# The y products of two scan chunks issued together, and one PSUM bank moved from the projections to y while the scan runs

## The chip, the cores and the metric

The kernel runs on one core of one Trainium2 chip. The metric is the device time of one execution in microseconds; where several runs are given, it is their median. The core has a matrix engine (TensorE, PE in the profile; its weight loads are listed apart as PEld), VectorE (DVE), ScalarE (ACT), GpSimd (POOL) and SyncE (SP), which here issues nearly all DMA transfers. Each engine takes its instructions in a fixed order and waits on semaphores. PSUM, into which TensorE writes, has eight banks of 512 fp32 columns by 128 partitions.

## The reference, cut to what matters

One inference step of a layer: 1024 prompt tokens and 8 decode tokens (1032 columns in all), D_MODEL 1024. One input projection gives z, the x/B/C channels of a Mamba-2 mixer, dt, a pooling input and two gates. The mixer's chunked scan is the part that the change touches (8 groups of 4 heads, head size 64, state size 128, 8 chunks of 128 tokens):

```python
def step(h, inp):
    xc, dtc, bc, cc = inp
    acum = jnp.cumsum(dtc * a_gr, axis=1)
    seg = acum[:, :, None] - acum[:, None, :]
    decay = jnp.exp(jnp.where(causal, seg, -jnp.inf))
    cb = jnp.einsum('bign,bjgn->bijg', cc, bc)
    m = cb[..., None] * decay * dtc[:, None]
    y = jnp.einsum('bijgr,bjgrp->bigrp', m, xc)
    y = y + jnp.einsum('bign,bgrpn->bigrp', cc, h) * jnp.exp(acum)[..., None]
    w_end = jnp.exp(acum[:, -1:] - acum) * dtc
    h_new = h * jnp.exp(acum[:, -1])[..., None, None] + jnp.einsum('bjgr,bjgn,bjgrp->bgrpn', w_end, bc, xc)
    return h_new, y
```

After the scan: a gated norm, a pooling branch, two branch projections merged by the gates, an output projection, and a SwiGLU FFN, with norms around both.

## The kernel before, in words

Activations lie transposed, channels on the partitions and tokens along the free axis. Every large product is done as three products of two-part operands (`mm3`, lines 229 to 232: wh by xh, wh by xl, wl by xh). A *unit* (`in_unit`) is one output block of 128 channels for one third of the tokens (344 columns): eight contraction tiles by three products, 24 matmuls into one PSUM bank with the tag "pj". Its bank is read out by ScalarE (and, for z, by VectorE as well).

The order of the work: the input norm and the pooling branch (four groups of two blocks, `pool_proj` and `pool_mix`, the latter with short units of six matmuls); then eight groups of projections (`group_proj`: B, C, x0, x1 with a causal convolution on VectorE, z0 and z1; 18 units per group); then the gates (48 units); then branches, output projection and FFN. `interleave` puts one step of the scan of group g-1 behind each unit of group g; the scan of the last group runs behind units of the gates.

The scan of a group (`ssd`) has 18 steps u. Step u=2c runs `stage1(c)`: three transposes and the product of B and C into a bank with the tag "T"; from it ScalarE copies BT, and VectorE makes xdt, wx and CB. The tile E of the chunk (128 by 4 by 128) is loaded by a DMA that SP issues (line 681), goes through ScalarE (lines 683 and 685) and is multiplied by CB on VectorE (line 686). Step u=2c+3 runs `stage2(c)`: the state product (line 703) and two products with the state of the chunk before (line 705) into the one bank "S", and the four y products (xdt of a head as weights, 64 columns; E of that head as moving operand; line 709) into the one bank "y". One y bank holds two chunks, an even one and the odd one behind it: it is taken at the even chunk, and VectorE reads it at the odd one (line 724, once for each of two blocks of 128 channels; GpSimd then adds the tile eA at line 728). In the trace each fp32 product is two instructions, so a chunk has 2 of line 703, 4 of line 705 and 8 of line 709.

The PSUM banks are fixed for the whole kernel: pj 4, T 2, S 1, y 1. The scan's SBUF tiles rotate over fixed numbers of buffers: E 3, all others 2, except a few small ones with 1. A new tile in a buffer waits for the last reader of the old one. The order of instructions on an engine is made by the framework's scheduler at build time, mostly that of the program, with later instructions moved up where its own timing model has a gap.

Of the kernel before, what the change touches and what calls it, by code (L numbers as in the profile page):

```python
# [8 lines left out]
F32 = mybir.dt.float32  # L9
# [4 lines left out]
PSUM = bass.MemoryType.PSUM  # L14
DRAM = bass.MemoryType.DRAM

P = 128
SEQ = 1024
NS = 8
T = SEQ + NS  # L20
# [4 lines left out]
R = 4  # L25
# [59 lines left out]
def layer_kernel(ctx: ExitStack, tc: tile.TileContext, xT, wi, wdt, wpool, wba, wbb, wo, wfi,  # L85
# [3 lines left out]
    sync, act, dve, pool, pe = nc.sync, nc.scalar, nc.vector, nc.gpsimd, nc.tensor  # L89
# [2 lines left out]
    rp = ctx.enter_context(tc.tile_pool(name="rp", bufs=NR))  # L92
    wp = ctx.enter_context(tc.tile_pool(name="wp", bufs=2))
    dram = ctx.enter_context(tc.tile_pool(name="scr", bufs=1, space=DRAM))
    ps = ctx.enter_context(tc.tile_pool(name="ps", bufs=2, space=PSUM))

    def row(n=T, dt=F32, name="row"):
        return rp.tile([P, n], dt, name=name, tag="R")

    def bank(tag):  # L100
        return ps.tile([P, 512], F32, name=tag, tag=tag, bufs={"pj": 4, "T": 2, "S": 1, "y": 1}[tag])

# [1 line left out]
    plan = []  # L104

    def want(key, src, n=1024, eng=dve, rows_=False, raw=None):
# [80 lines left out]
        w_dma()  # L187
        return raw

# [1 line left out]
    x_rows = [row(name="xrow") for _ in range(KT)]  # L191

    def load_x(th):
# [32 lines left out]
    def pcol(base, i):  # L226
        return ppt[:, base + i:base + i + 1]
# [3 lines left out]
        pe.matmul(out, wh, xl, start=False, stop=False)  # L231
        return pe.matmul(out, wl, xh, start=False, stop=stop)  # L232

# [1 line left out]
    def sum_cols(bk, src, toks=TOK, c0=0):  # L235
        for i, off in enumerate(toks):
            pe.matmul(bk[:, c0 + i:c0 + i + 1], src[:, off:off + P], ones[:, 0:1], start=True, stop=True)
# [28 lines left out]
    def rstd_bank(bk, scale, eps):  # L266
        return rstd_spread(rstd_diag(bk, scale, eps))

# [1 line left out]
    xh = [None] * KT  # L270
    xl = [None] * KT

# [11 lines left out]
    def in_rstd(sacc):  # L284
        bk = bank("T")
        sum_cols(bk, sacc)
        return rstd_diag(bk, 1.0 / 1024, eps1)
# [32 lines left out]
    def load_in(blk):  # L320
        return load_w("in", blk)

# [1 line left out]
    s_yb = dram.tile([KT, P, T], F32, name="s_yb")  # L324
    icnt = const.tile([P, 16], F32, name="icnt")
    for t in range(15):
# [94 lines left out]
                act.activation(out=yb[:, TH[th]], in_=pt[:, :W], func=AF.Copy, scale=pcol(PP_PSC, blk))  # L421
            sync.dma_start(out=s_yb[blk], in_=yb)

# [1 line left out]
    dtT = const.tile([P, 9, 32], F32, name="dtT")  # L425
    wend = const.tile([P, 8, 32], F32, name="wend")
    acT = const.tile([P, 8, 32], F32, name="acT")
# [102 lines left out]
    pend = pool_split(pool_group(0, us))  # L530
# [3 lines left out]
    pend = pool_split(pool_group(1, us))  # L534
# [3 lines left out]
    pend = pool_split(pool_group(2, us))  # L538
# [1 line left out]
    pool_mix(2, *pend)  # L540
    last_mix = pool_group(3, us)

# [1 line left out]
    s_y = dram.tile([16, P, T], F32, name="s_y")  # L544
    s_ga = dram.tile([KT, P, T], F32, name="s_ga")
    s_gb = dram.tile([KT, P, T], F32, name="s_gb")
# [2 lines left out]
    sp = ssd_ctx.enter_context(tc.tile_pool(name="sp", bufs=2))  # L549
# [90 lines left out]
    def b4x(ap, n):  # L640
        return ap.unsqueeze(2).broadcast_to([P, ap.shape[1], n])
# [4 lines left out]
    def ssd(g):  # L646
        d = grp[g]
        SB, SC, SX = d["B"], d["C"], (d["x0"], d["x1"])
        # B and C rows of the decode tokens, spread over the partitions through DRAM
        tb = bank("T")  # L650
        bcs = sp.tile([P, 2, NS], F32, name="bcs", tag="bcs", bufs=1)
        for i, S in enumerate((SB, SC)):
            pool.tensor_copy(out=bcs[:, i], in_=samples(S))
        pe.transpose(tb[:16, 0:P], bcs.rearrange("p a b -> p (a b)"), ident)
        bcr = sp.tile([16, P], F32, name="bcr", tag="bcr", bufs=1)
        act.copy(out=bcr, in_=tb[:16, 0:P])
        sync.dma_start(out=s_bc[g].rearrange("a (b n) -> (a b) n", n=P), in_=bcr)
        Y = [row(name="Y") for _ in range(2)]
# [1 line left out]
        pend = [None, None]  # L660
# [3 lines left out]
        def stage1(c):  # L664
            cs = slice(c * P, (c + 1) * P)
            tb = bank("T")
            pe.transpose(tb[:, 0:P], SB[:, cs], ident)
            pe.transpose(tb[:, P:2 * P], SX[0][:, cs], ident)
            pe.transpose(tb[:, 2 * P:3 * P], SX[1][:, cs], ident)
            pe.matmul(tb[:, 3 * P:], SB[:, cs], SC[:, cs], start=True, stop=True)  # L670
            BT = sp.tile([P, P], F32, name="BT", tag="BT")
            act.copy(out=BT, in_=tb[:, 0:P])
            xv = tb[:, P:3 * P].rearrange("p (r q) -> p r q", r=R)
            xdt = sp.tile([P, R, 64], F32, name="xdt", tag="xdt")
            dve.tensor_tensor(out=xdt, in0=xv, in1=b4x(dtT[:, c, hs], 64), op=ALU.mult)
            wx = sp.tile([P, R, 64], F32, name="wx", tag="wx")
            dve.tensor_tensor(out=wx, in0=xv, in1=b4x(wend[:, c, hs], 64), op=ALU.mult)
            CB = sp.tile([P, P], F32, name="CB", tag="CB")
            dve.tensor_tensor(out=CB, in0=tb[:, 3 * P:], in1=tri, op=ALU.mult)
            E = sp.tile([P, R, P], F32, name="E", tag="E", bufs=3)  # L680
            sync.dma_start(out=E, in_=s_ac[c, hs].unsqueeze(0).broadcast_to([P, R, P]))
            for h in range(R):
                act.activation(out=E[:, h], in_=E[:, h], func=AF.Relu, scale=-1.0,  # L683
                               bias=acT[:, c, 4 * g + h:4 * g + h + 1])
            act.activation(out=E, in_=E, func=AF.Exp, scale=-1.0)
            dve.tensor_tensor(out=E, in0=E, in1=CB.unsqueeze(1).broadcast_to([P, R, P]), op=ALU.mult)
            if c % 2 == 0:
                eA[0] = sp.tile([P, 2, 2, P], F32, name="eA", tag="eA")
                for r2 in range(2):
                    for c2 in range(2):  # L690
                        sync.dma_start(out=eA[0][r2 * 64:(r2 + 1) * 64, :, c2],
                                       in_=s_ea[c + c2, hs].rearrange("(a r) i -> r a i", r=2)[r2].unsqueeze(0)
                                       .broadcast_to([64, 2, P]))
            return BT, xdt, wx, eA[0], E

        def stage2(c, BT, xdt, wx, eA, E):
            hT = hst[0]
            if c % 2 == 0:
                pend[1] = bank("y")
            yb = pend[1]  # L700
            yv = yb.rearrange("p (a c i) -> p a c i", a=2, c=2)
            sb = bank("S")
            pe.matmul(sb[:, :256], BT, wx.rearrange("p r q -> p (r q)"), start=True, stop=True)
            for a in range(2 if c else 0):
                pe.matmul(sb[:, (2 + a) * P:(3 + a) * P], hT[:, 2 * a:2 * a + 2, :].rearrange("p r q -> p (r q)"),
                          SC[:, c * P:(c + 1) * P], start=True, stop=True)
            for h in range(R):
                o = yv[(h % 2) * 64:(h % 2) * 64 + 64, h // 2, c % 2, :]
                pe.matmul(o, xdt[:, h, :], E[:, h, :], start=True, stop=True)  # L709
            sv = sb[:, :256].rearrange("p (r q) -> p r q", r=R)  # L710
            hn = sp.tile([P, R, 64], F32, name="hT", tag="hT")
            if c == 0:
                act.copy(out=hn, in_=sv)
            else:
                pool.tensor_tensor(out=hn, in0=hT, in1=b4x(cd[:, c, hs], 64), op=ALU.mult)
                dve.tensor_tensor(out=hn, in0=hn, in1=sv, op=ALU.add)
            hst[0] = hn
            if c:
                dve.tensor_tensor(out=eA[:, :, c % 2], in0=eA[:, :, c % 2],
                                  in1=sb[:, 2 * P:].rearrange("p (a i) -> p a i", a=2), op=ALU.mult)  # L720
            if c % 2 == 1:
                for a in range(2):
                    s2 = slice((c - 1) * P, (c + 1) * P)
                    dve.scalar_tensor_tensor(out=Y[a][:, s2], in0=SX[a][:, s2], scalar=pcol(PP_D, 2 * g + a),
                                             in1=yb[:, a * 256:(a + 1) * 256], op0=ALU.mult, op1=ALU.add)
                    c2 = 1 if c == 1 else 0
                    s2 = slice((c - 1 + c2) * P, (c + 1) * P)
                    pool.tensor_tensor(out=Y[a][:, s2], in0=Y[a][:, s2],
                                       in1=eA[:, a, c2:].rearrange("p c i -> p (c i)"), op=ALU.add)
# [35 lines left out]
        for u in range(2 * NCH + 2):  # L765
            if u % 2 == 0 and u < 2 * NCH:
                st1[u // 2] = stage1(u // 2)
            if u >= 3 and u % 2 == 1:
                c = (u - 3) // 2
# [62 lines left out]
        interleave(group_proj(g), ssd(g - 1), 1)  # L832
    interleave(gates(), ssd(G - 1), 1)
    ssd_ctx.close()

# [1 line left out]
    lp = ctx.enter_context(tc.tile_pool(name="lp", bufs=4))  # L837

    def big(n=T, name="big", dt=F32):
# [50 lines left out]
        del qh, ql  # L890
    del m

# [1 line left out]
    s_h = dram.tile([KT, P, T], F32, name="s_h")  # L894
    sacc = ssacc
    mo = [[None] * 4, [None] * 4]
# [50 lines left out]
    B = [{}, {}]  # L947
# [79 lines left out]
                yield  # L1027
        mo[c] = None

# [1 line left out]
    s_act = dram.tile([NFF, P, T], F32, name="s_act")  # L1031

    def fill_units():
# [20 lines left out]
    sums = {}  # L1054
# [74 lines left out]
                dve.tensor_tensor(out=wk[:, H2:], in0=wk[:, H2:], in1=wk[:, :H2], op=ALU.mult)  # L1129
                sync.dma_start(out=s_act[j][:, chunk(c)], in_=wk[:, H2:])  # L1130

# [1 line left out]
    acc = [None] * KT  # L1133
    acts = {}

# [89 lines left out]
    side = None  # L1225
    for sl, toks in zip(LTH, ((0, 128, 256), (0, 128, 256), LTOK)):
        interleave(ffn_out(s, (sl,), True), side, 1)
        side = finish(sl, toks)
# [1 line left out]
        pass  # L1230


# [1 line left out]
_OUTS = {  # L1234
    "yT": (P, KT, T), "o_conv": (G, P, 4, 27), "o_ssmp": (G, P, 256), "o_ssms": (16, P, NS, P),
    "o_poolp": (P, KT, 15), "o_pools": (P, KT, NS, 15),
# [72 lines left out]
```

## Time and profile before

| what | value |
|---|---|
| runs (us) | 2146.68, 2149.07, 2152.36 |
| median (us) | 2149.07 |
| span of the profiled execution (us) | 2146.5 |
| PE busy, share of the span | 2091.0 us, 97% |
| DVE, ACT, POOL busy | 1361.0, 791.1, 406.9 us |
| mean granted TensorE clock | 0.993 |

The profiled execution is known by its span, from the first to the last instruction on the core, 2146.5 us; that is 0.2 us below the fastest of the three runs and 2.6 us below their median. PE counts as busy from a matmul's start to its modelled end, and matmuls overlap, so 97% doesn't say that the array works at its peak for 97% of the time; idle time of PE is real time lost, though.

### The profile page before, as it was taken

Reading aid. Unit: us, or ns where it says so; the run is one execution under the profiler, and the core shown is the slowest. Engines: PE = TensorE matmul, PEld = TensorE weight load, DVE = VectorE, ACT = ScalarE, POOL = GpSimd, SP = SyncE. Lnnn points to the kernel's source line nnn. Section 1 sums busy time; section 2 is a strip of 40 time slices with the busy share of each in tenths; the row PEclk is TensorE's granted clock in tenths of the full one; section 3 lists DMA queues with packets and bytes.
Section 4 is the critical chain, followed back from the end, with each engine's and each line's share of the span. In section 5 each row is a group of like instructions: output and inputs, shape, how many; then the busy total and the mean of one; then the engine's idle time right before and its main releaser. Section 6 shows DMA issues by size and latency. Waiting matters only on the chain.

```text
span 2146.5 us, 36509 instructions
## 1 busy us (share of the span) xinstructions
PE 2091.0 (97%) x14722; PEld 2055.9 (96%) x14722; DVE 1361.0 (63%) x2283; ACT 791.1 (37%) x1530; POOL 406.9 (19%) x407
## 2 busy tenths in 40 slices
PE   6999999999999999999999999989999999999997
PEld 5999999999999999999999999989999999999997
DVE  7665578677787776422155775679777666654436
ACT  5443344444444444233331024445333233351112
POOL 3100234424434243210100001352000000000004
PEclk9999999999999999999999999989999999999998
DMA  3332343334434334433343444234322222252133
GB/s 126 97 112 72 100 125 125 124 105 142 139 99 127 116 128 149 137 118 136 117 150 101 145 135 151 101 101 142 96 95 90 72 78 90 99 188 69 40 101 107
DMA packets 121961, 243.74 MB, mean 114 GB/s; under 512 B 24896, under 2 KB 62912, under 8 KB 121792
## 3 DMA queue, kind: packets, MB, share of 16 engines
q1 hardware_dynamic: 121360, 241.12, 35.0%
q8 instruction: 116, 1.90, 0.4%
q14 instruction: 53, 0.43, 0.1%
q10 hardware_dynamic: 432, 0.28, 0.0%
HBM read 189.38 MB, written 51.98 MB: 112 GB/s over the span
## 4 chain that ended last, share of the span: by engine, by line
PE 71%; DVE 8%; ACT 2%; DMA 2%; issue 2%; POOL 2%; SPq 0%; DVEq 0%; ACTq 0%; POOLq 0%
PE pj L230 20%; PE pj L232 20%; PE pj L231 20%; DVE S L595 2%; DMA E<-s_ac 1%; PE y L709 1%; PE y L230 1%; PE y L231 1%; PE y L232 1%; DVE S L597 1%; PE T L230 1%; PE T L232 1%; PE T L231 1%; PE S L231 1%; PE S L232 1%
## 5 line engine op out<-in xcount | busy, mean ns | idle before, releaser
L230 PE MATMUL pj<-xh,wh 128*128 128x344 f32 x1728 | 563.3, 327 | 2.4 <-ACT xh L299 2.4
L231 PE MATMUL pj<-xl,wh 128*128 128x344 f32 x1728 | 553.0, 320 | 0.1
L232 PE MATMUL pj<-xh,wl 128*128 128x344 f32 x1728 | 552.8, 320 | 0.0
L230 PEld LDWEIGHTS pj<-xh,wh 128*128 128x128 f32 x1728 | 324.9, 188 | 14.3 <-issue 11.0
L231 PEld LDWEIGHTS pj<-xl,wh 128*128 128x128 f32 x1728 | 325.5, 188 | 1.4 <-DVE xl L300 0.8
L232 PEld LDWEIGHTS pj<-xh,wl 128*128 128x128 f32 x1728 | 325.2, 188 | 0.0
L167 DVE TENSOR_TENSOR wl<-wr,wh 128x1024 fp32r<-128x1024 f32 (+1 forms) x125 | 170.4, 1364 | 210.0 <-ACT wh L166 210.0
L166 ACT CAST wh<-wr 128x1024 fp32r<-128x1024 f32 x142 | 146.6, 1033 | 363.4 <-PE pj L231 335.5
L917 POOL TENSOR_TENSOR ssacc<-ssacc,sq 128x258 f32<-128x258 f32 (+3 forms) x41 | 43.7, 1072 | 923.8 <-ACT sq L916 917.7
L230 PE MATMUL pj<-qh,wh 128*128 128x344 f32 (+1 forms) x608 | 189.7, 312 | 0.0
L231 PE MATMUL pj<-ql,wh 128*128 128x344 f32 (+1 forms) x608 | 189.7, 312 | 0.0
L232 PE MATMUL pj<-qh,wl 128*128 128x344 f32 (+1 forms) x608 | 189.6, 312 | 0.0
L231 PE MATMUL pj<-al,wh 128*128 128x344 f32 (+2 forms) x528 | 168.9, 320 | 0.0
L232 PE MATMUL pj<-ah,wl 128*128 128x344 f32 (+2 forms) x528 | 168.8, 320 | 0.0
L230 PE MATMUL pj<-ah,wh 128*128 128x344 f32 (+2 forms) x528 | 168.8, 320 | 0.0
L683 ACT ACTIVATE E<-E,acT 128x128 f32<-128x128 f32 x256 | 83.9, 393 | 214.8 <-DMA E<-s_ac 198.1
L595 DVE SCALAR_TENSOR_TENSOR S<-U,hcw,S 128x1056 f32<-128x1056 f32 x96 | 137.3, 1430 | 3.0 <-ACT S L593 2.9
L1172 DVE TENSOR_TENSOR acc<-acc,pj 128x344 f32<-128x344 f32 (+2 forms) x120 | 60.8, 510 | 98.0 <-PE pj L232 97.9
L231 PEld LDWEIGHTS pj<-ql,wh 128*128 128x128 f32 x608 | 114.4, 188 | 0.0
L232 PEld LDWEIGHTS pj<-qh,wl 128*128 128x128 f32 x608 | 114.4, 188 | 0.0
L230 PEld LDWEIGHTS pj<-qh,wh 128*128 128x128 f32 x608 | 114.3, 188 | 0.0
L232 PEld LDWEIGHTS pj<-ah,wl 128*128 128x128 f32 x528 | 99.3, 188 | 0.0
(351 smaller groups left out, 4898.1 us busy)
## 6 DMA issues: line engine op xcount, KB each, us to landing
wr<-wi SPq DMA_DIRECT2D x72, 512.0 KB, 4.3
E<-s_ac SPq DMA_DIRECT2D x64, 256.0 KB, 4.0
wr<-wfi SPq DMA_DIRECT2D x30, 512.0 KB, 3.6
s_act<-wk SPq DMA_DIRECT2D x44, 258.0 KB, 2.0
ar<-s_act SPq DMA_DIRECT2D x22, 516.0 KB, 4.7
wu<-wfi SPq DMA_DIRECT2D x22, 512.0 KB, 3.7
wr<-wfo SPq DMA_DIRECT2D x20, 512.0 KB, 3.7
s_y<-Y SPq DMA_DIRECT2D x16, 516.0 KB, 3.8
```

The source lines that it names most:

```text
L166: act.copy(out=wh, in_=raw)
L167: eng.tensor_tensor(out=wl, in0=raw, in1=wh, op=ALU.subtract)
L230: pe.matmul(out, wh, xh, start=start, stop=False)
L231: pe.matmul(out, wh, xl, start=False, stop=False)
L232: return pe.matmul(out, wl, xh, start=False, stop=stop)
L595: dve.scalar_tensor_tensor(out=S[:, :CW], in0=U[:, k:k + CW], scalar=tap(k), in1=S[:, :CW], op0=ALU.mult, op1=ALU.add)
L597: dve.scalar_tensor_tensor(out=S[:, :CW], in0=U[:, 0:CW], scalar=1.0, in1=S[:, :CW], op0=ALU.add, op1=ALU.mult)
L683: act.activation(out=E[:, h], in_=E[:, h], func=AF.Relu, scale=-1.0, bias=acT[:, c, 4 * g + h:4 * g + h + 1])
L709: pe.matmul(o, xdt[:, h, :], E[:, h, :], start=True, stop=True)
L917: eng.tensor_tensor(out=sacc[:, sl], in0=sacc[:, sl], in1=q, op=ALU.add)
L1172: dve.tensor_tensor(out=acc[ob][:, sl], in0=acc[ob][:, sl], in1=pt, op=ALU.add)
```

## The change

While the projections and the scan run, PSUM is divided as pj 3, T 2, S 1, y 2; when the gates are done that pool of banks is closed and another opened with the old division (pj 4, T 2, S 1, y 1). In `stage2` the y products of an even chunk are no longer issued at its own step: its xdt and E are kept, and all eight products of the two chunks are issued at the odd chunk's step, into a y bank that is taken there. xdt gets a third buffer; to make room, CB has one buffer instead of two, and the small tile bcr takes a buffer of the tag BT. The removed comment lines, which do nothing, are left out here.

```diff
-    ps = ctx.enter_context(tc.tile_pool(name="ps", bufs=2, space=PSUM))
+    ps_ctx = ExitStack()
+    ps = [ps_ctx.enter_context(tc.tile_pool(name="ps", bufs=2, space=PSUM))]
+    BANKS = [{"pj": 3, "T": 2, "S": 1, "y": 2}]
...
     def bank(tag):
-        return ps.tile([P, 512], F32, name=tag, tag=tag, bufs={"pj": 4, "T": 2, "S": 1, "y": 1}[tag])
+        return ps[0].tile([P, 512], F32, name=tag, tag=tag, bufs=BANKS[0][tag])
...
-        bcr = sp.tile([16, P], F32, name="bcr", tag="bcr", bufs=1)
+        bcr = sp.tile([P, P], F32, name="bcr", tag="BT")[:16]
...
-            xdt = sp.tile([P, R, 64], F32, name="xdt", tag="xdt")
+            xdt = sp.tile([P, R, 64], F32, name="xdt", tag="xdt", bufs=3)
...
-            CB = sp.tile([P, P], F32, name="CB", tag="CB")
+            CB = sp.tile([P, P], F32, name="CB", tag="CB", bufs=1)
...
         def stage2(c, BT, xdt, wx, eA, E):
             hT = hst[0]
-            if c % 2 == 0:
-                pend[1] = bank("y")
-            yb = pend[1]
-            yv = yb.rearrange("p (a c i) -> p a c i", a=2, c=2)
             sb = bank("S")
...
-            for h in range(R):
-                o = yv[(h % 2) * 64:(h % 2) * 64 + 64, h // 2, c % 2, :]
-                pe.matmul(o, xdt[:, h, :], E[:, h, :], start=True, stop=True)
+            if c % 2 == 0:
+                pend[0] = xdt, E
+            else:
+                yb = bank("y")
+                yv = yb.rearrange("p (a c i) -> p a c i", a=2, c=2)
+                for i, (x_, E_) in enumerate((pend[0], (xdt, E))):
+                    for h in range(R):
+                        o = yv[(h % 2) * 64:(h % 2) * 64 + 64, h // 2, i, :]
+                        pe.matmul(o, x_[:, h, :], E_[:, h, :], start=True, stop=True)
+                pend[0] = None
...
     interleave(gates(), ssd(G - 1), 1)
     ssd_ctx.close()
+    ps_ctx.close()
+    ps[0] = ctx.enter_context(tc.tile_pool(name="ps3", bufs=2, space=PSUM))
+    BANKS[0] = {"pj": 4, "T": 2, "S": 1, "y": 1}
```

## Rows read from the trace of the kernel before

**Rows 1.** Busy time by stretch: us, then each engine's busy time, PEclk, DMA share, GB/s.
```profile
60.00:220.00 160.00, 160.00 (x1016) 159.11 (x1015) 92.85 (x124) 64.76 (x116) 11.22 (x41) 1.00 0.32 92
220.00:916.00 696.00, 683.28 (x4641) 656.97 (x4641) 500.09 (x728) 305.87 (x675) 258.53 (x260) 1.00 0.39 125
```

**Rows 2.** Waits of PE, 220 to 920 us: total us, times, longest.
```profile
PE y L709 <- DVE Y L724: 12.2, 9, 1.6
PE S L703 <- DVE eA L719: 0.3, 1, 0.3
```

**Rows 3.** Timeline of PE, two undisturbed scan steps: start us, us, line, tiles, count.
```profile
249.03 0.27 PE L667 MATMUL T<-ident,S 128*128 128x128 f32 x1
249.14 0.27 PE L668 MATMUL T<-ident,S 128*128 128x128 f32 x1
...
249.50 0.40 PE L230 MATMUL pj<-xh,wh 128*128 128x344 f32 x1
249.74 0.32 PE L231 MATMUL pj<-xl,wh 128*128 128x344 f32 x1
249.90 0.32 PE L232 MATMUL pj<-xh,wl 128*128 128x344 f32 x1
...
253.36 0.59 PE L703 MATMUL S<-wx,BT 128*128 128x256 f32 x2
253.80 0.61 PE L705 MATMUL S<-S,hT 128*128 128x128 f32 x4
254.33 0.66 PE L709 MATMUL y<-E,xdt 128*64 128x128 f32 x8
254.92 0.42 PE L230 MATMUL pj<-xh,wh 128*128 128x344 f32 x1
255.18 0.32 PE L231 MATMUL pj<-xl,wh 128*128 128x344 f32 x1
```

**Rows 4.** The same timeline cut at 254.94 us: the last two y instructions.
```profile
254.71 0.28 PE L709 MATMUL y<-E,xdt 128*64 128x128 f32 x2
```

**Rows 5.** Timeline of PE, a step with the wait: [idle before, releaser].
```profile
448.92 0.61 PE L705 MATMUL S<-S,hT 128*128 128x128 f32 x4
451.12 0.66 PE L709 MATMUL y<-E,xdt 128*64 128x128 f32 x8 [1.59 <-DVE Y L724]
```

**Rows 6.** Timeline of DVE just before that step's y products.
```profile
448.84 1.75 DVE L597 SCALAR_TENSOR_TENSOR S<-U,S 128x1056 f32<-128x1056 f32 x1 [0.18 <-ACT U L596]
450.51 0.47 DVE L724 SCALAR_TENSOR_TENSOR Y<-S,ppt,y 128x256 f32<-128x256 f32 x1
```

**Rows 7.** The load of E: SP's waits (220 to 920 us); timelines of SP, ACT, PE.
```profile
SPq L681 <- PE y L709: 63.1, 24, 5.7
434.09 0.38 SPq L681 DMA_DIRECT2D E<-s_ac  x1
438.98 1.28 ACT L683 ACTIVATE E<-E,acT 128x128 f32<-128x128 f32 x4 [6.98 <-DMA E<-s_ac]
441.11 0.42 ACT L581 COPY U<-pj 128x336 f32<-128x336 f32 x1
444.10 0.41 PE L230 MATMUL pj<-xh,wh 128*128 128x344 f32 x1
```

**Rows 8.** Timelines of PE and ACT in the pooling branch, two places.
```profile
68.22 0.32 PE L230 MATMUL pj<-xh,wh 128*128 128x344 f32 x1
68.84 1.13 ACT L339 COPY U<-pj 128x344 f32<-128x344 f32 x3
112.09 0.32 PE L230 MATMUL pj<-dh,wh 128*128 128x344 f32 x1
112.52 0.44 ACT L339 COPY U<-pj 128x344 f32<-128x344 f32 x1
```

**Rows 9.** Timelines of PE and ACT where the gates end and the branches begin.
```profile
1032.59 0.32 PE L230 MATMUL pj<-qh,wh 128*128 128x344 f32 x1
1033.59 0.45 ACT L627 ACTIVATE gt<-pj 128x344 f32<-128x344 f32 x1
```

## The prediction

> **What bounds the kernel now.** I read the busy times by stretch first. While the scan runs (220 to 916 us) PE is busy for 683.3 of 696 us, and no other engine is near its limit: DVE 500 us, ACT 306, POOL 259. In the pooling branch before it PE is busy without a break, 160.0 of 160 [rows 1]. So PE sets the time in both stretches, and what the change is worth is the idle time it takes from PE or gives to it, and any slow stretch inside PE's own stream that "busy" doesn't show. Next, PE's waits: of the 12.7 us of idle in the scan 12.2 are nine waits of the y products for line 724, the read of the y bank by VectorE; the only other one listed is 0.3 us of the S products on line 719 [rows 2]. Then the timelines of such places.
>
> **Where the y wait comes from.** Undisturbed, the y products start 0.53 us behind the first instruction of line 705 (253.80 to 254.33) [rows 3]; in a step with the wait it is 2.20 us (448.92 to 451.12) [rows 5], so 1.67 us are lost, 0.08 more than the 1.59 that the view of waits counts, since matmuls overlap. The bank was filled by the odd chunk one step earlier and could have been read long before; but on VectorE the two reads of it do not stand together. A 1.75 us instruction of the next group's convolution (line 597) lies ahead of the second read, which starts at 450.51, ends at 450.98, and releases the y products of the next even chunk at 451.12 [rows 6, 5].
>
> **The change part by part.**
>
> *The y wait.* With the y bank taken at the odd chunk only, each pair's products come a whole chunk later relative to the read of the pair before, and with two banks they need only the read of the pair before that: some 40 us of room where a wait of at most 1.67 us was short. The nine waits go: 12.2 us plus nine times 0.08, that is -12.9 us. VectorE's order isn't cured by this, so what may be late next is the S bank, still one, which is read just before (line 719). In the kernel before this wait is 0.3 us in all [rows 2]. It can grow, because PE now reaches the fifth chunk of a group earlier by what two pairs save (2 x 0.34, below): between 0 and 7 x 0.7 = 4.9 us over the seven groups whose scan has convolutions beside it. I take +1.4, near the low end, since the row is near zero.
>
> *Fewer changes into and out of the y products.* The scan step with transposes is the measure of a clean switch: from 249.03 to the second projection matmul at 249.74 are 0.71 us, which is five instructions at 0.11 us (249.03 to 249.14) and one projection matmul at 0.16 (249.74 to 249.90). Nothing is left over [rows 3]. The step with y products is not clean. Four instructions of line 705 at 0.11 fill 253.80 to 254.24, but y starts at 254.33: 0.09 over. Eight y instructions in 0.59 us are 0.07 each, so they overlap, in pairs for the two column halves; the last pair starts at 254.71 [rows 4], 0.38 after the first, where three pitches of 0.11 are 0.33: 0.05 over. From the last pair to the second projection matmul (255.18) are 0.47 us, where 0.11 + 0.16 = 0.27 would do: 0.20 over. Together 0.34 us that a block of y products costs beyond its work [rows 3, 4]. Before there are 64 such blocks, after 32 of twice the length. If the 0.34 belongs to the block, 32 x 0.34 = -10.9 us; if it doubles with the block's length, 0. I take -10.9, because 0.29 of the 0.34 lies at the two ends of the block, in the handing over to and from instructions of another shape; half of it (-5.4) is the weak end of the range. The pages offer a reason: the Trainium skill (TensorEngine Tiling (Array Packing), Key Properties) states that a change of tiling mode, from 128 to 64 columns here, drains the engine. By that rule the cost is per change, and the sum would be the -10.9; that it is per product could be read from these rows as well, and no row here decides it.
>
> *Three banks for projections.* Now a unit waits for the read of the third unit before it, not the fourth. In the scan the tightest place of a group is the unit starting at 444.10: the third one before it is read until 441.53 (441.11 + 0.42) and a short copy of 8 columns behind [rows 7], so over 2 us are to spare. In the pooling branch two places have nothing to spare. The unit that starts at 68.22 is the third after the one whose copy is the first of those at 68.84; that copy ends 0.44 later, so PE stands for 69.28 - 68.22 = 1.06 us. The short unit at 112.09 is the third after the one read until 112.96: 0.87 us [rows 8]. PE has no idle time there that could take it up [rows 1]. With 0.1 for each hand-over: +2.2 us; below, 0 if ScalarE's new order puts these copies earlier; above, 4, if the short units behind each add as much again.
>
> *The second pool of banks.* Before, the first branch product starts at 1032.59 while the last gate unit is still being read until 1034.04 [rows 9]. If the new banks wait for all of the old ones, PE stands for 1.45 us; if only for the one they overlie, 0. I take +0.5.
>
> *Buffers.* CB with one buffer costs nothing: VectorE makes CB and uses it up in line 686 of the same step, in order, before the next. A third xdt buffer covers exactly the longer life of the even chunk's xdt. bcr in a BT buffer makes the second BT copy of a group wait until the 8 KB of bcr have landed; it is due a whole scan step after that store, and its own reader, the S product, comes two units later, so ScalarE may stand a little and PE doesn't see it.
>
> *E.* Its three buffers stay, but E of an even chunk is now read one step later. SP's issue of a later E already waits for y products, 63.1 us in 24 waits [rows 7], and more will wait. For the fifth E after the first (chunk 5) this is 434.09 before. Its buffer is now freed only when the y products of chunks 2 and 3 end: a step takes two units (2 x 24 x 0.16), 0.55 and 1.56, about 9.8 us, so that of chunk 3 lies at 448.92 + 0.53 - 9.8 = 439.6, and with 1.0 us of products the E can be issued at about 440.6. The kernel before needed 4.9 us from issue to ScalarE's start on it (434.09 to 438.98), so that start is at 445.5, some 6.5 us later than before. The y products of that chunk are two steps on and now come with the odd chunk's, so the lateness has cover, unless something stands behind it on ScalarE (the second rival). SP's own queue is held up until then too; behind the E there stands, as before, the next weight load, which waits for VectorE anyhow.
>
> **Sum.** -12.9 - 10.9 + 1.4 + 2.2 + 0.5 = -19.7 us. The sum is made against a span of 2146.5 us, 2.6 below the median of the runs; the same difference from the median gives 2149.07 - 19.7 = **2129.4 us**. Own range of this case: best -12.9 - 10.9 - 0.3, with no loss from the banks, is -24.1 or 2125; worst -12.9 - 5.4 + 4.9 + 4 + 1.5 is -7.9 or 2141.
>
> **The rivals.** *The wait moves to the S bank.* For it: VectorE is as late as before, and the S products already wait for line 719, which stands just ahead of line 724 on VectorE. Against: in the waiting step S was on time to 0.3 us [rows 2], and what is late, line 597, stands behind line 719. If all 12.9 come back there: -10.9 + 2.2 + 0.5 = -8.2, 2141 us.
>
> *ScalarE stands for the E that comes later, and the kernel gets slower.* The mechanism is visible: ScalarE stood 6.98 us for this load, and the read of a projection bank (441.11) and the start of the next convolution were queued behind it [rows 7]. If that order stays, the read moves by 6.5 us to end at 448.0, while with three banks the unit of 444.10 needs it: PE stands 3.9 us per group; the convolution chain on VectorE is late by the other 2.6 at the S bank. Over seven groups 7 x 6.5 = 45, so 2149.1 - 19.7 + 45 = 2175 us. It decides from 19.7 / 7 = 2.8 us per group on. Against: the order is made anew at build time, with the E's wait for the y products in it, and the unit whose read would be stuck ends a unit before those y products; so the read should now stand ahead of the E and gain, for the 6.98 us go too.
>
> *The block's cost doubles with its length.* Then the second part is nothing: -12.9 + 1.4 + 2.2 + 0.5 = -8.8, 2140 us.
>
> *Both the first and the third.* The change then doesn't do what it says: +2.7 us, 2152, within 0.3%.
>
> **How the numbers follow.** A change under about 0.3% (6.4 us) can't be told from none by these runs, which lie 5.7 us apart. Chances: the forecast 0.64; the S bank 0.08; the block's cost 0.07; both 0.09; ScalarE and the E 0.12. The first three are faster by over 0.3% (the ends of the second and third, at 8 us, partly within it): faster 0.77, same 0.11, slower 0.12. The range of 2122 to 2147 takes in the forecast's own range, with 3 us more below for idle time on VectorE that PE's earlier arrival may use, and the two cases at 2140 and 2141 with as much spread above; it leaves out the slow case and most of the case of both.
>
> **What would show it.** In the profile after: no wait of the y products on line 724; 32 y blocks of 16 instructions, each with about 1.0 us from its first to the next projection matmul, and even chunks' S products followed by projections without surplus; waits of the S products on line 719 of a few us at most; new waits of a projection matmul on line 339 or 421 near 69 and 113 us, about 2 us in all, and none on lines 579 to 582, 610 or 611 in the scan; ScalarE's waits for E no longer ahead of line 581. Wrong would be: projection matmuls in the scan waiting for ScalarE; a y block that takes twice the old 0.59 plus its surplus; or another order of the engines in the later stages (output projection, FFN) that costs or saves several us there, where this change has no part.

## The result, and the profile after

| | before | after |
|---|---|---|
| median of the runs on one chip (us) | 2147.88 (2146.42 to 2152.36) | 2125.36 (2123.95 to 2125.54) |
| span of the profiled execution (us) | 2146.5 | 2123.5 |
| mean granted TensorE clock | 0.993 | 0.993 |

Before has a fourth run here, beside the three that the prediction knew. The ratio is 0.9886 (95% interval 0.987 to 0.9902): the kernel is 22.5 us faster, where 19.7 were forecast (2129.4 us). By stage, from the starts of the same matmuls in both traces, the span's 23.0 us are:

| stage | after less before (us) | forecast (us) |
|---|---|---|
| input norm | +1.4 | 0 |
| pooling branch | +2.4 | +2.2 |
| scan, with the gates behind its end | -25.5 | -22.4 |
| start of the branches | +1.5 | +0.5 |
| output projection and FFN | -2.8 | 0 |

The busy times by stretch of the kernel after, in the columns of [rows 1] (PE's come behind the stretch and its length):

```profile
60.00:220.00 160.00, 158.02 (x1000) 156.68 (x999) 92.78 (x124) 64.25 (x115) 12.08 (x42) 1.00 0.32 94
220.00:894.00 674.00, 674.00 (x4665) 659.75 (x4664) 514.08 (x727) 312.25 (x677) 249.74 (x259) 1.00 0.41 129
```

In the scan PE has no idle time left, where 12.7 us stood in [rows 1]. The pooling branch now has 2.0 of it and the branches' start 1.3. These two rows are all of PE's waits from 60 to 1300 us; there is none for y or S, which [rows 2] had:

```profile
PE pj L232 <- ACT U L341: 2.0, 2, 1.0
PE pj L232 <- ACT gt L629: 1.3, 1, 1.3
```

The same three in the timeline of PE, at the places of [rows 8, 9]:

```profile
70.73 0.42 PE L232 MATMUL pj<-xh,wh 128*128 128x344 f32 x1 [0.94 <-ACT U L341]
...
115.89 0.43 PE L232 MATMUL pj<-dh,wh 128*128 128x344 f32 x1 [1.03 <-ACT U L341]
...
1012.36 0.43 PE L232 MATMUL pj<-qh,wh 128*128 128x344 f32 x1 [1.34 <-ACT gt L629]
```

Two scan steps of the kernel after in the timeline of PE, an even chunk's and the odd chunk's behind it, to be read beside the step of [rows 3]:

```profile
424.75 0.59 PE L701 MATMUL S<-wx,BT 128*128 128x256 f32 x2
425.18 0.61 PE L703 MATMUL S<-S,hT 128*128 128x128 f32 x4
425.54 0.41 PE L232 MATMUL pj<-xh,wh 128*128 128x344 f32 x1
425.79 0.32 PE L233 MATMUL pj<-xl,wh 128*128 128x344 f32 x1
...
433.73 0.59 PE L701 MATMUL S<-wx,BT 128*128 128x256 f32 x2
434.16 0.61 PE L703 MATMUL S<-S,hT 128*128 128x128 f32 x4
434.70 1.09 PE L713 MATMUL y<-E,xdt 128*64 128x128 f32 x16
435.72 0.43 PE L232 MATMUL pj<-xh,wh 128*128 128x344 f32 x1
435.99 0.32 PE L233 MATMUL pj<-xl,wh 128*128 128x344 f32 x1
```

The working of the prediction can be repeated on them. The odd step: four instructions of line 703 (line 705 before) at 0.11 would let y start at 434.60, it starts 0.10 later; eight pairs of y at 0.11 and one projection matmul at 0.16 are 1.04 us, and from 434.70 to 435.99 are 1.29, so 0.25 more. Together 0.35, as the block of half the length had 0.34 [rows 3, 4]. The even step has no such block: from 425.18 to 425.79 are 0.61, and 4 x 0.11 + 0.16 is 0.60.

### The profile page after: what moved, and what is told of

Read it like the earlier page. It is cut to its first block, busy times and chain, and to the rows that moved or that the text cites. A ratio compares the mean times of both kernels' runs of the same rounds, so it can differ in the third digit from the quotient of the medians.

```text
span 2123.5 us, 36521 instructions
## 1 busy us (share of the span) xinstructions
PE 2078.0 (98%) x14722; PEld 2054.6 (97%) x14722; DVE 1375.0 (65%) x2283; ACT 796.6 (38%) x1530; POOL 394.0 (19%) x407
## 4 chain that ended last, share of the span: by engine, by line
PE 92%; DVE 5%; issue 1%; DMA 1%; ACT 1%; POOL 1%; SPq 0%; DVEq 0%; ACTq 0%; POOLq 0%
PE pj L232 26%; PE pj L234 26%; PE pj L233 26%; PE y L713 2%; PE S L701 1%; PE S L703 1%; PE y L232 1%; PE y L233 1%; PE y L234 1%; PE T L232 1%; PE T L233 1%; PE T L234 1%; PE S L233 1%; PE S L234 1%; PE S L232 1%
## 5 line engine op out<-in xcount | busy, mean ns | idle before, releaser
L233 PEld LDWEIGHTS pj<-al,wh 128*128 128x128 f32 x528 | 99.3, 188 | 0.0
```

## The experiments

The theory after the result had two halves: each block of y products costs PE about 0.35 us beyond its work, whatever its length, and PE's waits for VectorE went because the y products of a pair no longer need the bank just read. The rivals: the saving is PSUM's (a second y bank), or it hangs on the order of the other engines. For each run the kernel before was timed again on the same chip, and the ratio is to that; microseconds above or below the change or another run are differences of medians that were not taken side by side. The scan's length below is the time from the start of the first transpose to that of the last, 64 of them; the view of that line gives, for the kernel before and then after (first and last start behind the durations):

```profile
L667 PE MATMUL T<-ident,S x64: 270/271/273, 221.8 to 900.0; 128*128 128x128 f32 x64
```

```profile
L669 PE MATMUL T<-ident,S x64: 270/271/273, 225.7 to 878.6; 128*128 128x128 f32 x64
```

That is 678.2 and 652.9 us.

**e1, pairs with the old banks.** The change without its banks: y products in pairs, PSUM as before in the whole kernel, in one pool.

```diff
-    ps_ctx = ExitStack()
-    ps = [ps_ctx.enter_context(tc.tile_pool(name="ps", bufs=2, space=PSUM))]
-    BANKS = [{"pj": 3, "T": 2, "S": 1, "y": 2}]
+    ps = [ctx.enter_context(tc.tile_pool(name="ps", bufs=2, space=PSUM))]
+    BANKS = [{"pj": 4, "T": 2, "S": 1, "y": 1}]
...
-    ps_ctx.close()
-    ps[0] = ctx.enter_context(tc.tile_pool(name="ps3", bufs=2, space=PSUM))
-    BANKS[0] = {"pj": 4, "T": 2, "S": 1, "y": 1}
```

> The y products of two chunks issued together as in the change, but PSUM divided as before (pj 4, T 2, S 1, y 1) from beginning to end, no second pool of banks. Theory (the gain is the nine waits plus half of the block costs, and the banks only cost): the scan keeps all of its 25 us, because one y bank taken at the odd chunk has two scan steps of room for its read; the two waits of about 1 us in the pooling branch and the one of 1.3 us at the branches go; 2125.4 - 3.3 = about 2121.5 us. Rival (the second y bank is what takes the wait away): the y products wait for line 724's successor again, up to 13 us, 2130 to 2138 us.

Measured: 2120.44 us, ratio 0.9861 (0.9845 to 0.9876), so 28.5 us faster than before and about 5 faster than the change. The scan takes 653.0 us (223.3 to 876.3), as long as that of the change to 0.1 us, with one y bank. The busy times by stretch of e1:

```profile
60.00:220.00 160.00, 160.00 (x1015) 159.04 (x1014) 92.78 (x124) 64.79 (x116) 12.15 (x42) 1.00 0.33 94
220.00:892.00 672.00, 672.00 (x4652) 657.75 (x4651) 514.53 (x727) 311.94 (x677) 250.01 (x259) 1.00 0.41 129
```

PE has no idle time in either stretch, and waits for nothing from there to 1300 us. So the second y bank gives nothing once the products come in pairs, and the third projection bank taken for it and the second pool cost 2.4 and 1.5 us.

**e2, the banks alone.** The banks of the change, with y products at every chunk, and the small buffers, as before.

```diff
+            if c % 2 == 0:
+                pend[1] = bank("y")
+            yb = pend[1]
+            yv = yb.rearrange("p (a c i) -> p a c i", a=2, c=2)
...
-            if c % 2 == 0:
-                pend[0] = xdt, E
-            else:
-                yb = bank("y")
...
+            for h in range(R):
+                o = yv[(h % 2) * 64:(h % 2) * 64 + 64, h // 2, c % 2, :]
+                pe.matmul(o, xdt[:, h, :], E[:, h, :], start=True, stop=True)
```

> The banks alone: pj 3 and y 2 while the scan runs, the old division after, but each chunk's y products at its own step as before the change. Theory: the nine waits go (-12.9, and some -1.4 of short S waits around them), the 64 blocks of y products stay, and the three banks cost 2 + 1.3 us: 2147.9 - 14.3 + 3.5 = about 2137 us, with no PE wait in the scan. Rival (VectorE stays late and PE meets it at the S bank, one instruction pair earlier): waits of the S products of several us, 2142 to 2150 us.

Measured: 2149.08 us, ratio 1.0 (0.9989 to 1.0011). The theory missed, and the rival came: waits of the S products. PE's waits in the scan of e2:

```profile
PE S L705 <- DVE eA L721: 5.6, 6, 2.2
PE S L705 <- ACT wh L168: 2.6, 6, 0.6
```

No wait of y is left, so the second bank does what a second bank can; but PE now stands at the S products (line 705 here), one instruction group earlier, for VectorE's read of the one S bank. That holds for the second row too, though it names ScalarE's cast: in all twelve places the S products start 0.15 us behind the end of a read on line 721. The scan takes 677.0 us, 1.2 less than before. In the place of [rows 5 to 7], timelines of ACT and then of PE in e2:

```profile
440.86 1.28 ACT L685 ACTIVATE E<-E,acT 128x128 f32<-128x128 f32 x4 [6.97 <-DMA E<-s_ac]
...
442.99 0.43 ACT L583 COPY U<-pj 128x336 f32<-128x336 f32 x1
```

```profile
450.30 0.67 PE L705 MATMUL S<-wx,BT 128*128 128x256 f32 x2 [1.11 <-DVE eA L721]
```

ScalarE stands 6.97 us for an E with the read of a projection bank queued behind it, just as before (6.98 and then 441.11 in [rows 7]). That row was the new suspect. The 8.2 us listed are not all that these waits cost. Behind the longest one, 2.2 us in which PE stood idle, PE ran at half the clock (1.2 GHz) for 3.4 us, by the granted clock (PEclk, 0.50) of that stretch:

```profile
799.60:803.00 3.40, 3.40 (x15) 2.67 (x16) 3.22 (x7) 3.40 (x9) 1.67 (x3) 0.50 0.00 0
```

**e3, two blocks again.** The change, with the even chunk's products ahead of the S products of the odd step and the odd chunk's behind them: the same number of products, two blocks a pair.

```diff
...
+                def ys(i, x_, E_):
+                    for h in range(R):
+                        o = yv[(h % 2) * 64:(h % 2) * 64 + 64, h // 2, i, :]
+                        pe.matmul(o, x_[:, h, :], E_[:, h, :], start=True, stop=True)
+                ys(0, *pend[0])
             sb = bank("S")
...
+                ys(1, xdt, E)
```

> As the change, but in the odd step the even chunk's y products stand ahead of the S products and the odd chunk's behind them: the same products in the same step, in 64 blocks of 8 instructions in place of 32 of 16. Theory (0.35 us belong to each block, whatever its length): 32 x 0.35 = 11.2 us more than the change, 2136.5 us, with no wait on PE in the scan. Rival (the cost goes with the number of products): no difference, 2125.4 us.

Measured: 2135.78 us, ratio 0.9937 (0.9922 to 0.9952), 10.4 above the change; its scan takes 664.3 us, 11.4 more. PE in an odd step of e3:

```profile
436.00 0.66 PE L707 MATMUL y<-E,xdt 128*64 128x128 f32 x8
436.59 0.70 PE L710 MATMUL S<-wx,BT 128*128 128x256 f32 x2
437.12 0.61 PE L712 MATMUL S<-S,hT 128*128 128x128 f32 x4
437.66 0.66 PE L707 MATMUL y<-E,xdt 128*64 128x128 f32 x8
438.25 0.43 PE L232 MATMUL pj<-xh,wh 128*128 128x344 f32 x1
438.51 0.32 PE L233 MATMUL pj<-xl,wh 128*128 128x344 f32 x1
```

From 437.66 to 438.51 are the 0.85 us of [rows 3], and the block ahead of S pays its own entry and exit. Over all pairs the median odd step is 0.35 us longer than the change's (2446 ns less 2096, each beyond the projections' own pitch): 32 x 0.35 = 11.2 us. The cost is one per block.

**e4, products of full width.** The change, with two heads' xdt side by side as 128 columns of weights in every y product, so that the second head of a pair overwrites the first and y is wrong in half.

```diff
-                        o = yv[(h % 2) * 64:(h % 2) * 64 + 64, h // 2, i, :]
-                        pe.matmul(o, x_[:, h, :], E_[:, h, :], start=True, stop=True)
+                        w2 = x_[:, h // 2 * 2:h // 2 * 2 + 2, :].rearrange("p r q -> p (r q)")
+                        pe.matmul(yv[:, h // 2, i, :], w2, E_[:, h, :], start=True, stop=True)
```

> As the change, but each y product takes the columns of both heads of its pair as weights (128 columns in place of 64), into the same bank; the second head of a pair overwrites the first, so half of y comes from the wrong head's E and the output isn't the reference's. Theory (the cost of a block comes with the narrower instructions, at its two ends): no surplus, but the products no longer overlap in pairs: 16 x 0.107 = 1.71 us per block in place of 0.86 + 0.39 = 1.25, so 32 x 0.46 = 14.8 us more, about 2140 us. Rival (the surplus is the price of coming from the S products, or of waiting on E, whatever the shape): it stays as well, 32 x 0.85 = 27 us more, about 2152 us.

Measured: 2142.07 us, ratio 0.9963 (0.995 to 0.9976), 16.7 above the change, where the theory had 14.8 and the rival 27. An odd step of e4 on PE:

```profile
439.70 0.61 PE L703 MATMUL S<-S,hT 128*128 128x128 f32 x4
440.14 1.95 PE L713 MATMUL y<-E,xdt 128*128 128x128 f32 x16
441.85 0.40 PE L232 MATMUL pj<-xh,wh 128*128 128x344 f32 x1
442.09 0.32 PE L233 MATMUL pj<-xl,wh 128*128 128x344 f32 x1
```

Products of 64 columns run in pairs and products of 128 one by one, so the work of the block is 16 x 0.11 = 1.76 in place of 0.88; the entry is clean (439.70 to 440.14 is 4 x 0.11), and from 440.14 to 442.09 are 1.95, where 1.76 + 0.16 = 1.92 would do. Over all pairs the median odd step takes 1.79 us more than the even one (2663 ns less 878), which is 0.112 for each of the 16, as they follow each other within the block. So nothing of the 0.35 is left, and the surplus belongs to the step between 128 and 64 columns and not to y, its bank or its operands.

**e5, the kernel before with two E buffers.** This makes each E come later, so that the scheduler, which orders by its own timing, may place the work on it otherwise.

```diff
-            E = sp.tile([P, R, P], F32, name="E", tag="E", bufs=3)
+            E = sp.tile([P, R, P], F32, name="E", tag="E", bufs=2)
```

> The kernel before the change with one number changed: E has 2 buffers in place of 3, so that the load of a chunk's E waits for the y products of the chunk two before it, which is about as late as the change makes it for every second E. Theory (the waits of y and S come from VectorE's convolution being late, because ScalarE stands for an E that was put ahead of the reading of a projection bank; an E that is known to come later is put behind it): the waits go with nothing else changed, 2148.9 - 13 = about 2136 us. Rival (a later E is only later): ScalarE's waits for E grow, the waits on line 724 stay or grow, 2149 us or more.

Measured: 2138.66 us, ratio 0.9964 (0.9952 to 0.9977), faster with a buffer less, but the theory had all waits go. The scan takes 670.4 us, 7.8 less. PE's waits in the scan of e5, where before had 12.2 in nine [rows 2]:

```profile
PE y L709 <- DVE Y L724: 5.6, 5, 1.6
```

ScalarE in the place of [rows 7]:

```profile
434.59 1.28 ACT L683 ACTIVATE E<-E,acT 128x128 f32<-128x128 f32 x4 [5.66 <-DMA E<-s_ac]
...
436.71 0.43 ACT L581 COPY U<-pj 128x336 f32<-128x336 f32 x1
```

So an E stands ahead of the read here too, and in all seven groups, though another one: the E of the chunk before (chunk 4, not 5), which the same edit makes late. It is done somewhat sooner than the E of before was, and the read with it.

**e6, e1 with two E buffers.** The same edit as e5's, made in e1.

> The y products in pairs with the old banks (as e1), E with 2 buffers in place of 3: both E's of a pair are loaded only when the pair before is done. Theory (the y products have some 7 us of cover over E's way from its load through ScalarE and VectorE, and the whole way is about 10 us in four scan steps of nearly 10 each): the same time as e1, 2120 us. Rival (ScalarE stands for E's that come together, with reads of projection banks behind): waits of projection matmuls or of y on VectorE's line with CB, 2125 to 2150 us.

Measured: 2119.84 us, ratio 0.9873 (0.9859 to 0.9886); the scan takes 653.0 us (222.0 to 875.0) and PE waits for nothing. The E that comes later has cover.

**e7 and e8, e1 with four E buffers, and its control.** The other way round: an earlier E could bring the old order back. On top of e1's edits, to make room, one buffer of the pool "rp" was given up (NR 36 to 35), so e8 has that edit alone.

```diff
-NR = 36
+NR = 35
...
-            E = sp.tile([P, R, P], F32, name="E", tag="E", bufs=3)
+            E = sp.tile([P, R, P], F32, name="E", tag="E", bufs=4)
```

> The y products in pairs with the old banks (as e1), E with 4 buffers, and 35 in place of 36 of the large rows to make room; to be held against e8, which has the 35 rows alone. Theory: with four buffers the fifth E again is free to load before the y products of its neighbours, goes ahead of the reading of a projection bank on ScalarE, and VectorE is late again: S products wait on line 719's successor by 1 us or more in most groups, 5 to 10 us over e8. Rival (it is the pairing or the y bank itself that took the waits away): no difference to e8.

> The control of e7: as e1 with 35 large rows. No theory has a reason for more than 1 to 3 us over e1: 2120 to 2123 us.

Measured: e7 2120.66 us, ratio 0.9878 (0.9862 to 0.9893); e8 2121.76, ratio 0.9881 (0.9867 to 0.9894). There is no difference, where 5 to 10 us were expected: a miss. ScalarE in e7 at that place:

```profile
424.83 0.63 ACT L686 ACTIVATE E<-E 128x512 f32<-128x512 f32 x1
...
426.94 0.43 ACT L582 COPY U<-pj 128x336 f32<-128x336 f32 x1
```

With four buffers the E came early enough to be finished (425.46) before the read's turn came (426.94), so there was nothing to stand for. More buffers did no harm by themselves here. Since e5 and e7 change the order only indirectly, the next pair sets it.

**e9, the kernel before with ScalarE's order set.** Only this: the first activations on an E are issued behind the latest start of a convolution, so that they can't stand ahead of a projection bank's read that this convolution needs. One y bank, y products at every chunk.

```diff
-            act.activation(out=S[:, :CW], in_=U[:, 0:CW], func=AF.Identity, scale=tap(0), bias=hcw[:, cb:cb + 1])
+            conv[0] = act.activation(out=S[:, :CW], in_=U[:, 0:CW], func=AF.Identity, scale=tap(0),
+                                     bias=hcw[:, cb:cb + 1]).ins
...
-            for h in range(R):
-                act.activation(out=E[:, h], in_=E[:, h], func=AF.Relu, scale=-1.0,
-                               bias=acT[:, c, 4 * g + h:4 * g + h + 1])
+            with tc.issue_after(conv[0]):
+                for h in range(R):
+                    act.activation(out=E[:, h], in_=E[:, h], func=AF.Relu, scale=-1.0,
+                                   bias=acT[:, c, 4 * g + h:4 * g + h + 1])
```

> The kernel before the change, with one order on ScalarE and nothing else: the work on a chunk's E is put behind the first convolution instruction of the latest projection block in the program, and so behind the reading of that block's last bank. Theory (the waits on lines 724 and 719 come from ScalarE standing for E ahead of that reading): the read of the third block's last unit moves from about 7.6 to about 1.5 us behind the fifth chunk's transposes, and the waits of y and S go: 2148.5 - 13 = 2135 us, with one y bank and 64 blocks. Rival (the one y bank, whose second read VectorE puts behind a convolution instruction, is enough for the wait): waits of y remain at 8 us or more, 2143 to 2149 us.

Measured: 2131.86 us, ratio 0.9917 (0.99 to 0.9934), and 664.0 us for the scan (223.3 to 887.3), 14.2 less than before. PE has no wait in it. By names and shapes, PE and GpSimd run the instructions of before in the same order; on VectorE 28 of 2283 stand elsewhere, none of them a read of the y bank or line 599. ScalarE and then VectorE in the place of [rows 6, 7]:

```profile
431.95 0.43 ACT L582 COPY U<-pj 128x336 f32<-128x336 f32 x1
432.55 1.27 ACT L594 ACTIVATE S<-U,hcw 128x1056 f32<-128x1056 f32 x1
433.73 1.27 ACT L686 ACTIVATE E<-E,acT 128x128 f32<-128x128 f32 x4
```

```profile
439.58 0.48 DVE L727 SCALAR_TENSOR_TENSOR Y<-S,ppt,y 128x256 f32<-128x256 f32 x1
440.22 1.77 DVE L599 SCALAR_TENSOR_TENSOR S<-U,S 128x1056 f32<-128x1056 f32 x1 [0.16 <-ACT U L598]
441.91 0.47 DVE L727 SCALAR_TENSOR_TENSOR Y<-S,ppt,y 128x256 f32<-128x256 f32 x1
```

The long instruction of the convolution (line 599, line 597 before) still lies between the two reads of the y bank; it starts at 440.22 in place of 448.84 [rows 6], so the second read is done long before PE comes back.

**e10, the banks alone with ScalarE's order set.** e2 with the edit of e9.

> The banks alone (as e2), with the same order on ScalarE as e9. Theory: the waits of the S products that e2 had instead of those of y go, the banks cost their 3.5 us: 2149 - 10 = 2137 to 2140 us, 2 to 4 us over e9. Rival: the S bank stays the place where PE meets VectorE, as in e2, 2147 to 2150 us.

Measured: 2134.09 us, ratio 0.992 (0.9904 to 0.9935); scan 664.1 us (224.0 to 888.1). The S waits of e2 are gone with the same edit. What PE waits for from 60 to 1300 us in e10 is what the banks cost:

```profile
PE pj L232 <- ACT gt L631: 1.3, 1, 1.3
PE pj L232 <- ACT U L341: 0.9, 1, 0.9
```

With ScalarE's order set, the second y bank changes the scan by 0.1 us. The kernel's median is 2.2 us above e9's, the size of these two waits, but the six runs of either spread over more than that (2131.0 to 2139.0 and 2131.6 to 2137.8).

## Why the prediction was right, and where its reasons failed

**Fewer blocks: right, in mechanism and size.** -10.9 was forecast; a pair of chunks takes 878 + 2096 = 2974 ns beyond the projections' pitch, where two unstalled steps of before took 2 x 1662 = 3324, so 0.35 x 32 = 11.2 us. The open question, per block or per product, is settled by e3 (two blocks again: the 11.2 are back) and e4 (full width: all of the surplus gone). So the rival that doubled the cost with the length falls. The rule of the Trainium skill (TensorEngine Tiling (Array Packing), Key Properties), that changing the tiling mode drains the engine, agrees with both: the cost goes with the change between 128 and 64 columns.

**The y wait: right in size, wrong in cause, and this step failed.** The prediction put the wait down to one y bank and to VectorE's order, which "isn't cured by this", and let a small rest (+1.4) move to the S bank. e2 shows what the banks do without the pairs: the wait moves to S as the first rival had it, and nothing is gained. e9 shows what removes it: with one y bank, 64 blocks and VectorE's order between the two reads as it was, ScalarE's order alone takes away every wait and 14.2 us of the scan. So VectorE's instruction was not in the wrong place, it was late, since ScalarE stood for an E ahead of the read of a projection bank. That the size came out all the same is in part luck: another mechanism took the same waits away. The row was there to be read [rows 7], and was used only for a loss that the change might bring (the second rival), though it was already costing PE 14 us.

The change gets these 14 us too, and its order is another one, as the timeline of ACT shows:

```profile
430.40 0.43 ACT L583 COPY U<-pj 128x336 f32<-128x336 f32 x1
431.00 1.27 ACT L595 ACTIVATE S<-U,hcw 128x1056 f32<-128x1056 f32 x1
...
439.05 1.28 ACT L685 ACTIVATE E<-E,acT 128x128 f32<-128x128 f32 x4 [0.56 <-DMA E<-s_ac]
```

Here the read (430.40) and the start of the convolution stand ahead of the E (439.05); before, the E (438.98) stood ahead of the read (441.11). A measure of it is the time from PE's first transpose of a group's fifth chunk to the end of that read, over the seven groups: 7.04 to 7.65 us before and 7.39 to 9.55 in e2, where PE stands for about as much; 1.42 to 2.48 after, 1.42 to 1.45 in e1 and 1.43 in e9, where it stands for nothing. In e5 the groups differ, and the waits of y on PE's timeline follow the read (the list above leaves out the shortest):

| end of the read in e5, in order (us) | 5.06 | 5.68 | 6.26 | 6.32 | 6.43 | 7.23 | 7.36 |
|---|---|---|---|---|---|---|---|
| wait of y in that group (us) | 0 | 0.13 | 0.75 | 0.79 | 0.91 | 1.58 | 1.59 |

The change holds each E's buffer until the pair's y products, which SP's waits show (63.1 us in [rows 7]):

```profile
SPq L683 <- PE y L713: 115.4, 23, 9.9
```

That this is what made the scheduler put the E behind the read is argued from the later loads alone; e5 bears it out only in part, since there the E of chunk 5 went behind the read and that of chunk 4, late as well, was left ahead of it. ScalarE's waits for the load of E in the scan fell from 191.1 us before to 102.4 after.

And VectorE in the kernel after reads the bank long before it is needed, with line 599 still between:

```profile
437.86 0.47 DVE L729 SCALAR_TENSOR_TENSOR Y<-S,ppt,y 128x256 f32<-128x256 f32 x1
438.52 1.75 DVE L599 SCALAR_TENSOR_TENSOR S<-U,S 128x1056 f32<-128x1056 f32 x1 [0.19 <-ACT U L598]
440.18 0.47 DVE L729 SCALAR_TENSOR_TENSOR Y<-S,ppt,y 128x256 f32<-128x256 f32 x1
```

The prediction's argument against its second rival (the order is made anew, and the read should stand ahead of the E) was thus the main gain and not a footnote. Whether pairs with one y bank would also lose the waits if ScalarE kept the old order was not shown: e7 was meant to bring that order's wait back and didn't. For the S products e2 speaks against it, because they come at every chunk in the change as well.

**The S bank: sign wrong, by little.** +1.4 was forecast. The unstalled steps and the blocks explain 11.2 of the scan's 25.5 us; the remaining 14.3 are the waits, 12.9 for y and so about 1.4 for S, of which the list of [rows 2] shows 0.3. The timeline of before shows the others: in four of the steps with the wait the S products start 0.16 to 0.45 us later than in [rows 3]. The S waits went too, so the term is -1.4.

**Three projection banks: right.** +2.2 forecast, +2.4 measured, as 0.94 and 1.03 at the two places named.

**The second pool: at the top of its bounds.** +0.5 was taken from 0 to 1.45; it is +1.5, with a wait of 1.34. PE starts 0.05 us behind the end of the last gate unit's read, as it would if the new banks waited for all of the old ones; that it waited for more than the bank below is not shown.

**E and the buffers: right.** PE stood for none of them. Behind the fifth chunk's transposes the next E is issued at 5.99 us where it was 0.22 before (the group of [rows 7]): 5.8 later, where 6.5 was worked out. e6 makes E later still and loses nothing.

**What was not in the sum.** The input norm's +1.4: 1.2 of it lie between 23.9 and 26.7 us (last section). They are in e1 and in e9, which has no edit in that stage, and mostly not in e2 and e3 (+0.7 and +0.1 in all of the norm), so they aren't the change's. The last stages' -2.8 is a sign of being wrong that the prediction had named, if another order came with it; but there all engines run the same instructions in the same order as before, by names and shapes. The same difference is -2.1 in e2, -5.1 in e1 and -0.1 in e9. Why is open; no run was made for it. The terms that missed were -2.8 (S), +0.2, +1.0, +1.4, -2.8 and -0.3 (blocks), together -3.3, which is what lies between -19.7 and the span's -23.0.

## What to carry to other kernels

Where a matmul waits for a bank, follow the reader's lateness back through the other engines before giving it a second bank: here another bank only moved the wait to the next bank (ratio 1.0), while setting what an idle engine may stand for gave 0.9917 without touching the bank. Matmuls of fewer columns cost here at each change to and from full ones, so put them in few blocks: it is a saving on an engine that shows as 100% busy, and is seen only by adding up pitches. The best of these versions is the change without its banks (e1, 2120.44 us; e6 to e8, 2119.84 to 2121.76, can't be told from it): of two edits made together, each needs its own run.

## What the runs showed of the hardware that was not expected

A block of 64-column matmuls among 128-column ones costs 0.35 us beyond its work (0.10 at its start, 0.25 up to the second full matmul behind it), with 8 instructions or 16 alike, and nothing that can be told where the same products have 128 columns (1.95 us from the first of them to that second matmul, where 1.92 would do).

TensorE came to full speed in the input norm at different times in executions whose work there is the same. One such matmul in the timelines of PE, after and then before:

```profile
25.60 0.49 PE L234 MATMUL pj<-xh,wl 128*128 128x344 f32 x1
```

```profile
25.35 0.31 PE L232 MATMUL pj<-xh,wl 128*128 128x344 f32 x1
```

It takes 0.49 us in the one and 0.31 in the other. Such matmuls follow each other at 0.29 us until 26.7 us in the kernel after and at 0.16 from 23.9 us on in the kernel before, a difference of 1.2 us. These are the moments at which the record of the granted clock in either trace begins, with full speed; for the time ahead of them it holds nothing, and the column PEclk shows 1.00 there all the same. The pace is that of half the clock (1.2 GHz): e8 has a recorded stretch of it among the same matmuls, at 0.49 us each and 0.29 apart, shown by its busy times and one of them:

```profile
35.50:38.90 3.40, 3.40 (x14) 3.40 (x13) 3.40 (x7) 1.62 (x4) 1.30 (x2) 0.50 0.00 0
```

```profile
36.79 0.49 PE L233 MATMUL pj<-xh,wl 128*128 128x344 f32 x1
```

Ahead of full speed PE ran these matmuls one behind the other in both kernels, from 20.56 us after and from 20.37 us before. The record begins with full speed at 24.3 to 26.8 us in e1 to e4 and e9 as well; what sets the moment is open.
